# A two-block transformer forward pass: norms' root by Ln, Exp and Newton along the row, two projections around the row sum, and the last GLA head's norm by columns

## The chip, the cores and the metric

One core of one Trainium2 chip runs the kernel in one launch. The metric is device time in microseconds (us); lower is better. The core has TensorE (PE: matmuls, with PEld for loading their stationary operand), VectorE (DVE), ScalarE (ACT: activation functions from tables that are loaded by set), GpSimd (POOL), and DMA queues that SyncE (SP) issues to. TensorE's clock has two levels, 1.2 and 2.4 GHz; the profile's granted clock gives it as a share of the higher.

## The reference

512 tokens of width 1024 pass through two models of two layers each: gated linear attention (GLA) and a convolutional FFN, then native sparse attention (NSA) and a convolutional FFN, a norm, then twice a hybrid of differential and stick-breaking attention and a plain gated FFN, then a last norm. What the change touches is the norm of a vector, with n = 1024 for x, 256 for a head of the GLA, 128 for one of differential attention:

```python
def rmsnorm(x, g):
    x32 = x.astype(jnp.float32)
    y = x32 * lax.rsqrt(jnp.mean(x32 * x32, axis=-1, keepdims=True) + EPS)
    return (y * g).astype(x.dtype)
...
    o = o * lax.rsqrt(jnp.mean(o * o, axis=-1, keepdims=True) + EPS) * g_out      # GLA, per head
    o = o.reshape(Bsz, S, H * DV).astype(h.dtype) * jax.nn.silu(r)
    return o @ w_o
...
    h2 = rms_norm(x, g_ffn)                                                       # plain FFN
    gate, up = jnp.split(h2 @ w_ffn_in, 2, axis=-1)
    return x + (jax.nn.silu(gate) * up) @ w_ffn_out
```

## The kernel before

The residual x lies in SBUF as eight tiles of 128 channels by 512 tokens. Everything is fp32, split into a high and a low part in a reduced format (`hh`/`hl` for x times the norm's gain, `wh`/`wl` for a weight tile `wr`), and a product is three matmuls: high by high (L323), high weight by low data (L324), low weight by high data (L325). A projection to 128 channels is `proj` (L337): 8 blocks of x, 24 matmuls of 128x512 into one PSUM tile `pd`. The weight tiles come by DMA in the order of their use (`wblk`, `wrun`, `_wload`), three raw tiles and three pairs of split ones in flight (PF and WB are 3): ACT casts the high part (L199), DVE subtracts the low one (L200).

A norm's gain goes into `split_norm` ahead of the projection; the root of each token is multiplied in behind it, as `rbc`, a tile whose rows are all the same. So the projections of a norm can run before its root is there, but no output can be evicted without `rbc`. Before the change the root has two forms:

- by columns, for every norm of x: `sqsum` (L409) makes the squares on ACT (L415) and adds them on DVE (L419); `tok_sums` (L422, matmuls L425) sums over the channels, so that a token is a row of a 128x4 tile; `newton` (L396) takes the root in ten operations on DVE (`ms`, `ny`, `nt`: L444, L401 to L406); `bcast` (L427, matmuls L432) turns the columns to `rbc`, which ACT copies out (L435). `rstd` and `rms` put these together.
- by row, for a head of the GLA and of differential attention: `row_rstd` (L447) sums with one matmul (L453, two passes in the profile) so that every row holds the sums, and ACT takes Ln (L455), Exp (L456) and Square (L458), DVE two operations of one Newton step (L459, L460).

`gla` (L605) and `ffn` (L469) start with the norm and one projection ahead (`ahead`), written before the broadcast; `final` (L562) does the last down projection in two halves of 256 tokens, with the last norm by columns for each half (L588, L591, L595, L598), and multiplies the halves (L601). In `gla`, `hnorm` (L702) norms each head's output, then the gate's projections go through Silu (L757, only after the last head's Exp), the product is split (`ohh`, `ohl`), and the output projection follows. The low-rank decay of the GLA passes L629, L630 (`alow`) and the matmul L639.

Instructions are not run in the order in which they are written: a list scheduler with a model of the engines' times fixes each engine's row when the kernel is built, and PSUM banks are given out with it; `after` (L1189) adds an edge that it must keep. At run time each engine takes its row in that order. The rows of engines below are shown as they then stand; a wait in brackets names the engine or DMA queue that a row waits for, and numbers at names only tell tiles apart.

## Time and profile before

| | us |
|---|---|
| median of three runs (lowest, highest) | 2818.37 (2818.32, 2819.44) |
| the profiled execution | 2818.62 |
| its span, first to last instruction | 2816.5 |
| TensorE busy | 2764.6 |
| VectorE busy | 2013.6 |
| ScalarE busy | 1363.8 |
| GpSimd busy | 616.9 |

The profile is of one execution. A timeline row gives the start of an instruction or of a run of like ones, the time from the first's start to the last's end, the engine, the line, the tiles it writes and reads and their shapes; in brackets stands the idle time of the engine before it and what ended that. A matmul's own time overlaps the next one's, so distances between starts count: 0.227 us for 128x512 at 2.4 GHz, 0.43 at 1.2 GHz.

### The profile page before, as it was taken

The numbers are of one execution on the slowest core, as the hardware profiler recorded it, in microseconds if no ns is written. First come the engines' busy times: TensorE is split into PE (matmuls) and PEld (weight loads), VectorE is DVE, ScalarE is ACT, GpSimd is POOL, SyncE is SP. The second block draws the span as 40 slices with busy tenths as digits, with TensorE's granted clock in tenths as the row PEclk, the third lists the DMA queues.
The fourth block names the chain that finished last, engine by engine and source line by source line (L and its number), as shares of the span: only waits on it lengthen the run. The fifth ranks groups of instructions, "written<-read, shape, count | busy, mean of one in ns | idle before, by whom it ended". The sixth has DMA issues, their size and how long they took to land.

```text
span 2816.5 us, 39011 instructions
## 1 busy us (share of the span) xinstructions
PE 2764.6 (98%) x14592; PEld 2339.5 (83%) x14592; DVE 2013.6 (71%) x3105; ACT 1363.8 (48%) x2496; POOL 616.9 (22%) x513
## 2 busy tenths in 40 slices
PE   8999999999999999999999999999999999999998
PEld 6888888888777788888788887899988878889997
DVE  7656755754798875575689768787858896687786
ACT  5444433433486643344477734343436775443333
POOL 4500000001543100000400002466414000056551
PEclk9999999999999999999999999999999999999999
DMA  5222333234621123332422132333323223323331
GB/s 193 68 75 82 98 99 96 98 90 132 155 68 35 61 90 98 97 96 84 117 86 68 60 131 86 98 105 113 113 60 105 76 68 105 120 83 98 105 99 44
DMA packets 102124, 264.55 MB, mean 94 GB/s; under 512 B 13472, under 2 KB 17184, under 8 KB 101936
## 3 DMA queue, kind: packets, MB, share of 16 engines
q1 hardware_dynamic: 101936, 262.07, 29.8%
q8 instruction: 115, 1.88, 0.3%
q14 instruction: 73, 0.60, 0.1%
HBM read 237.93 MB, written 2.10 MB: 85 GB/s over the span
## 4 chain that ended last, share of the span: by engine, by line
PE 89%; DVE 6%; ACT 3%; issue 1%; POOL 1%; DMA 0%; SPq 0%; DVEq 0%; ACTq 0%; POOLq 0%
PE pd L323 20%; PE pd L324 20%; PE pd L325 20%; PE q L323 4%; PE q L325 4%; PE q L324 4%; PE pt L886 2%; PE q L373 1%; PE q L372 1%; PE q L371 1%; PE pa L682 1%; DVE wl L200 1%; DVE ptl L890 1%; PE po L1104 1%; PE pa L871 1%
## 5 line engine op out<-in xcount | busy, mean ns | idle before, releaser
L323 PE MATMUL pd<-hh,wh 128*128 128x512 f32 x1520 | 604.8, 398 | 0.9 <-ACT rbc L435 0.7
L325 PE MATMUL pd<-hh,wl 128*128 128x512 f32 x1520 | 600.7, 395 | 0.0
L324 PE MATMUL pd<-hl,wh 128*128 128x512 f32 x1520 | 600.6, 395 | 0.0
L200 DVE TENSOR_TENSOR wl<-wr,wh 128x1024 fp32r<-128x1024 f32 x309 | 386.3, 1252 | 48.2 <-ACT wh L199 43.3
L199 ACT CAST wh<-wr 128x1024 fp32r<-128x1024 f32 x309 | 320.8, 1045 | 142.2 <-PE pd L324 125.7
L379 DVE TENSOR_TENSOR xl<-yr,xh 128x512 fp32r<-128x512 f32 x322 | 324.4, 1018 | 41.4 <-ACT xh L378 39.8
L323 PEld LDWEIGHTS pd<-hh,wh 128*128 128x128 f32 x1520 | 289.3, 190 | 61.0 <-ACT wh L199 1.5
L325 PEld LDWEIGHTS pd<-hh,wl 128*128 128x128 f32 x1520 | 288.3, 190 | 59.9 <-issue 1.2
L324 PEld LDWEIGHTS pd<-hl,wh 128*128 128x128 f32 x1520 | 289.0, 190 | 58.4 <-issue 0.8
L323 PE MATMUL q<-bbh,xh 128*128 128x256 f32 x952 | 269.4, 283 | 1.5 <-ACT xh L378 1.5
L325 PE MATMUL q<-bbh,xl 128*128 128x256 f32 x952 | 269.4, 283 | 0.0
L324 PE MATMUL q<-bbl,xh 128*128 128x256 f32 x952 | 269.3, 283 | 0.0
L378 ACT CAST xh<-yr 128x512 fp32r<-128x512 f32 x356 | 203.0, 617 | 109.6 <-POOL yr L250 49.2
L773 POOL TENSOR_TENSOR rcos<-al,rbc 128x512 f32<-128x512 f32 x3 | 3.3, 1094 | 931.2 <-ACT rbc L435 931.2
L553 DVE TENSOR_TENSOR x<-pd,x 128x512 f32<-128x512 f32 x84 | 57.6, 689 | 208.3 <-PE pd L325 208.3
L323 PEld LDWEIGHTS q<-bbh,xh 128*128 128x128 f32 x952 | 182.6, 192 | 2.7 <-ACT xh L378 2.0
L324 PEld LDWEIGHTS q<-bbl,xh 128*128 128x128 f32 x952 | 182.6, 192 | 1.0
L325 PEld LDWEIGHTS q<-bbh,xl 128*128 128x128 f32 x952 | 182.6, 192 | 0.8
L275 POOL TENSOR_TENSOR tb<-hn 128x256 f32<-128x256 f32 x8 | 8.1, 1013 | 625.9 <-DVE hn L489 624.5
L324 PE MATMUL pd<-ffl,wh 128*128 128x512 f32 x352 | 136.9, 389 | 0.0
L325 PE MATMUL pd<-ffh,wl 128*128 128x512 f32 x352 | 136.9, 389 | 0.0
L323 PE MATMUL pd<-ffh,wh 128*128 128x512 f32 x352 | 136.3, 389 | 0.0
(402 smaller groups left out, 6138.2 us busy)
## 6 DMA issues: line engine op xcount, KB each, us to landing
wr<-wp SPq DMA_DIRECT2D x309, 512.0 KB, 3.5
yr<-ws SPq DMA_DIRECT2D x136, 256.0 KB, 2.8
yr<-wp SPq DMA_DIRECT2D x118, 256.0 KB, 2.9
sw<-blk SPq DMA_DIRECT2D x80, 64.0 KB, 2.0
x<-xT SPq DMA_DIRECT2D x8, 256.0 KB, 5.2
yr<-cmp_k SPq DMA_DIRECT2D x4, 512.0 KB, 6.4
yr<-cmp_v SPq DMA_DIRECT2D x4, 512.0 KB, 6.9
sw<-qs SPq DMA_DIRECT2D x32, 64.0 KB, 2.0
```

The costliest lines, as they stand in the source:

```text
L199: nc.scalar.copy(hi, raw)
L200: nc.vector.tensor_tensor(lo, raw, hi.bitcast(F), op=OP.subtract)
L323: ins = mm(ps, wh, xh, start=first, stop=False)
L324: mm(ps, wh, xl, start=False, stop=False)
L325: mm(ps, wl, xh, start=False, stop=last)
L371: mm(ps, hh[k][:, tk], wh, start=k == 0, stop=False)
L372: mm(ps, hh[k][:, tk], wl, start=False, stop=False)
L373: mm(ps, hl[k][:, tk], wh, start=False, stop=k == KB - 1)
L378: self.nc.scalar.copy(hi, x)
L379: (eng or self.nc.vector).tensor_tensor(lo, x, hi.bitcast(F), op=OP.subtract)
L553: nc.vector.tensor_tensor(x[n], ps, x[n], op=OP.add)
L886: nc.tensor.transpose(pt[:n, i * P:(i + 1) * P], x, self.ident)
```

## The change

- `row_rstd` takes a finished sum of squares and serves every norm: one matmul with -1, Ln, Exp, Square on ACT, two operations on DVE; no columns, no broadcast. Its matmul is remembered as `last_sum`.
- `columns` makes the token columns (sums and `newton`) beside it only where a token column is needed: `gla` (for v), `rms` in `nsa` and `hyb`. The FFNs need none.
- `headed` starts `gla` and `ffn`: projection 0, the row sum, projection 1, where projection 1's first matmul must come after the sum on TensorE.
- In `hnorm` the heads 0 to 2 keep the row form; the last head goes by columns and broadcast. The gate's Silus now wait for head 2's Exp and the last Exp of the decays (`last_exp`).
- `exp_ln_tables` is called at a head behind a Silu or Sigmoid, in `nsa` and in `final`, and puts the set of Ln and Exp in place. ACT's row has 18 table loads, 11 before.
- `final` takes the row form for each half. Constants move: a tile `minus`, gains without their factor.

```diff
-    def proj(self, name, layer, h, col, tag="pd"):
+    def proj(self, name, layer, h, col, tag="pd", prev=None):
 
         ps = self.psum(tag)
         hh, hl = h
         n = len(hh)
         for k in range(n):
             wh, wl = self.wblk((name, layer, k, col))
-            self.mm3(ps, wh, wl, hh[k], hl[k], k == 0, k == n - 1)
+            ins = self.mm3(ps, wh, wl, hh[k], hl[k], k == 0, k == n - 1)
+            if k == 0 and prev is not None:
+                self.after(ins, prev)
...
+    def row_rstd(self, acc, n, name="rbc", tag="pt"):
+
+
+        nc = self.nc
+        w = acc.shape[1]
+        ps = self.psum(tag)[:, :w]
+        self.last_sum = nc.tensor.matmul(ps, self.minus.to_broadcast([P, P]), acc, start=True, stop=True)
+        y, t = self.g(name)[:, :w], self.g("sq")[:, :w]
+        nc.scalar.activation(y, ps, AF.Ln, scale=-1.0 / n, bias=self.eps)
+        self.root = nc.scalar.activation(y, y, AF.Exp, scale=-0.5)
+        nc.scalar.activation(t, y, AF.Square, scale=(2 * n) ** -0.5)
+        nc.vector.scalar_tensor_tensor(t, ps, -EPS * n, t, op0=OP.add, op1=OP.mult)
+        nc.vector.scalar_tensor_tensor(y, t, 1.5, y, op0=OP.add, op1=OP.mult)
+        return y
...
+    def columns(self, acc, n=D, tag="pt"):
+
+        nc = self.nc
         ps = self.psum(tag)
-        nc.tensor.matmul(ps, self.ones.to_broadcast([P, P]), self.sqsum(xs), start=True, stop=True)
-        y = self.g("ob")
-        nc.scalar.activation(y, ps, AF.Ln, scale=1.0 / n, bias=self.eps)
-        self.root = nc.scalar.activation(y, y, AF.Exp, scale=-0.5)
-        t = self.g("sq")
-        nc.scalar.activation(t, y, AF.Square)
-        nc.vector.scalar_tensor_tensor(t, ps, EPS * n, t, op0=OP.add, op1=OP.mult)
-        nc.vector.scalar_tensor_tensor(y, t, -3.0 * n, y, op0=OP.add, op1=OP.mult)
-        return y
-
-    def rms(self, xs, n=D, name="rbc", tag="pt"):
-
-        y = self.rstd(xs, n, tag)
-        return y, self.bcast([y[:, t:t + 1] for t in range(4)], name, tag)
+        self.tok_sums(acc, ps)
+        a = self.sp.tile([P, 4], F, tag="ms", name="ms", bufs=3)
+        nc.vector.tensor_scalar(a, ps[:, 0:4], 1.0 / n, EPS, op0=OP.mult, op1=OP.add)
+        return self.newton(a, 4)
+
+    def rms(self, xs):
+
+        acc = self.sqsum(xs)
+        r = self.row_rstd(acc, D)
+        return self.columns(acc), r
+
+    def headed(self, x, *ahead):
+
+        if self.last_silu is not None:
+            self.exp_ln_tables()
+        acc = self.sqsum(x)
+        ps = [self.proj(*ahead[0])]
+        r = self.row_rstd(acc, D)
+        ps.append(self.proj(*ahead[1], prev=self.last_sum))
+        return acc, r, ps
...
-        ycol = self.rstd(x)
-        ahead = self.proj(w_up, layer, h, 0)
-        rbc = self.bcast([ycol[:, t:t + 1] for t in range(4)])
+        _, rbc, ahead = self.headed(x, (w_up, layer, h, 0), (w_up, layer, h, FB * P))
...
-                    ps = self.proj(w_up, layer, h, n * P) if n else ahead
+                    ps = ahead.pop(0) if ahead else self.proj(w_up, layer, h, n * P)
...
     def final(self, x, xn, gh, gl, w_down, layer, gname):
 
         nc = self.nc
+        self.exp_ln_tables()
         acc = self.sqsum(xn)
...
-            ps = self.psum("pt")
-            for t in range(2):
-                nc.tensor.matmul(ps[:, t:t + 1], acc[:, a * W + t * P:a * W + (t + 1) * P], self.ones,
-                                 start=True, stop=True)
-            v = self.sp.tile([P, 2], F, tag="fs", name="fs", bufs=2)
-            nc.vector.tensor_scalar(v, ps[:, 0:2], 1.0 / D, EPS, op0=OP.mult, op1=OP.add)
-            y = self.newton(v, 2)
-            ps = self.psum("pt")
-            for t in range(2):
-                nc.tensor.matmul(ps[:, t * P:(t + 1) * P], y[:, t:t + 1].to_broadcast([P, P]), self.ident,
-                                 start=True, stop=True)
-            r = self.g("rbc")[:, :W]
-            nc.scalar.copy(r, ps[:, :W])
+            r = self.row_rstd(acc[:, hs], D)
...
+        acc, rbc, ahead = self.headed(x, ("gla_w_in", 0, h, 0), ("gla_w_in", 0, h, 512))
+        ycol = self.columns(acc)
...
         def hnorm(hd):
-            ob = self.row_rstd(outs[2 * hd:2 * hd + 2], "pa")
+            acc = self.sqsum(outs[2 * hd:2 * hd + 2])
+            if hd < H - 1:
+                ob = self.row_rstd(acc, 256, "ob", "pa")
+            else:
+
+                y = self.columns(acc, 256, "pa")
+                ob = self.bcast([y[:, t:t + 1] for t in range(4)], "ob", "pa")
             for dv in range(2):
                 n = hd * 2 + dv
-                nc.vector.scalar_tensor_tensor(outs[n], outs[n], gain[:, n:n + 1], ob, op0=OP.mult, op1=OP.mult)
+                nc.vector.scalar_tensor_tensor(outs[n], outs[n], self.v("gla_norm", 0, n), ob,
+                                               op0=OP.mult, op1=OP.mult)
...
-            nc.scalar.activation(kd, kd, AF.Exp, scale=-1.0 / 16)
+            last_exp = nc.scalar.activation(kd, kd, AF.Exp, scale=-1.0 / 16)
...
-            self.after(nc.scalar.activation(t, t, AF.Silu), self.root)
+            self.last_silu = nc.scalar.activation(t, t, AF.Silu)
+            self.after(self.last_silu, self.root)
+            self.after(self.last_silu, last_exp)
...
     def nsa(self, x):
         nc = self.nc
         W = 4 * NCMP
+        self.exp_ln_tables()
         ycol, rbc = self.rms(x)
...
-            ob = self.row_rstd([o], "po")
+            ob = self.row_rstd(self.sqsum([o]), P, "ob", "po")
...
             self.after(ins, self.root)
+            self.last_silu = ins
```

In the kernel after, lines have moved: L323 to L325 are L325 to L327, L199/L200 are L201/L202, L425/L432/L435 are L429/L436/L439, L453 to L460 are L457 to L463.

The head of layer 1's conv FFN, TensorE's row. Before, from the last matmuls of projections 0 (`pd_8651`) and 1 (`pd_8695`) to the broadcast:

```order
L324 MATMUL pd_8695<-hl_8602,wh_8504 128x512
L325 MATMUL pd_8695<-hh_8601,wl_8505 128x512
L324 MATMUL pd_8651<-hl_8606,wh_8466 128x512 [waits DVE_49]
L325 MATMUL pd_8651<-hh_8605,wl_8467 128x512
L323 MATMUL pd_8695<-hh_8605,wh_8504 128x512
L425 MATMUL pt_8609<-al_71,sq_8610 128x1 [waits DVE_49]
L425 MATMUL pt_8609<-al_71,sq_8610 128x1 x3
L324 MATMUL pd_8695<-hl_8606,wh_8504 128x512
L325 MATMUL pd_8695<-hh_8605,wl_8505 128x512
L432 MATMUL pt_8682<-al_71,ny_8639 128x128 [waits DVE_49]
L432 MATMUL pt_8682<-al_71,ny_8639 128x128 x3
```

After, from the last matmuls of projection 0 (`pd_8639`) into projection 1 (`pd_8679`):

```order
L326 MATMUL pd_8639<-hl_8608,wh_8472 128x512 [waits DVE_49]
L327 MATMUL pd_8639<-hh_8607,wl_8473 128x512
L325 MATMUL pd_8639<-hh_8611,wh_8472 128x512 [waits Activation_49]
L326 MATMUL pd_8639<-hl_8612,wh_8472 128x512 [waits DVE_49]
L327 MATMUL pd_8639<-hh_8611,wl_8473 128x512
L457 MATMUL pt_8670<-sq_8616,minus_109 128x512 [waits DVE_49]
L325 MATMUL pd_8679<-hh_8583,wh_8510 128x512
L326 MATMUL pd_8679<-hl_8584,wh_8510 128x512
```

Before, the two projections are interleaved, and the last `hl` is used near the end of both; after, projection 0 runs to its end, then comes the sum, then projection 1.

The end of the GLA, ScalarE's row. Before, around the Ln and Exp of the last head (`ob_1409`), the table load and the gate's Silus (`gr`):

```order
L199 CAST wh_1616<-wr_1614 128x1024 [waits DMAHW3_49,PE_49]
L199 CAST wh_1655<-wr_1653 128x1024 [waits DMAHW4_49,PE_49]
L455 ACTIVATE ob_1409<-pa_1402,eps_107 128x512 [waits PE_49]
L456 ACTIVATE ob_1409<-ob_1409 128x512 [waits Activation_49]
L757 ACT_TABLE_LOAD
L757 ACTIVATE gr_1449<-gr_1449 128x512
L757 ACTIVATE gr_1488<-gr_1488 128x512
L757 ACTIVATE gr_1527<-gr_1527 128x512
L757 ACTIVATE gr_1566<-gr_1566 128x512
```

After, around those of head 2 (`ob_1349`); `sq_1404` is a square of the last head:

```order
L459 ACTIVATE ob_1349<-pa_1347,eps_107 128x512 [waits PE_49]
L762 COPY go_1392<-po_1384 128x512 [waits PE_49]
L460 ACTIVATE ob_1349<-ob_1349 128x512 [waits Activation_49]
L771 ACT_TABLE_LOAD
L771 ACTIVATE gr_1468<-gr_1468 128x512
L771 ACTIVATE gr_1507<-gr_1507 128x512
L771 ACTIVATE gr_1546<-gr_1546 128x512 [waits DVE_49]
L771 ACTIVATE gr_1585<-gr_1585 128x512 [waits DVE_49]
L461 ACTIVATE sq_1350<-ob_1349 128x512 [waits Activation_49]
L419 ACTIVATE sq_1404<-go_1392 128x512
L201 CAST wh_1596<-wr_1594 128x1024 [waits DMAHW2_49,PE_49]
```

The table load and the first four Silus have moved in front of the last head's squares.

The head of the first plain FFN, ScalarE's row around the root (`rbc`). Before, with the copy of the broadcast:

```order
L378 CAST xh_15341<-yr_15337 128x512 [waits DMAHW7_49,PE_49]
L378 CAST xh_15345<-yr_15339 128x512 [waits DMAHW0_49,Activation_49]
L199 CAST wh_14947<-wr_14945 128x1024 [waits PE_49]
L435 COPY rbc_14980<-pt_14975 128x512 [waits PE_49]
L533 ACT_TABLE_LOAD
L533 ACTIVATE tp_14982<-tp_14982 128x512 [waits DVE_49]
L265 CAST bbh_15033<-hn_15029 128x256 [waits DVE_49]
```

After, with Ln, Exp and Square (`wh_14961` takes the buffer of `wh_14801`, projection 1's):

```order
L459 ACTIVATE rbc_14951<-pt_14949,eps_107 128x512 [waits PE_49]
L382 CAST xh_15272<-yr_15268 128x512 [waits DMAHW4_49]
L382 CAST xh_15276<-yr_15270 128x512 [waits DMAHW5_49]
L382 CAST xh_15311<-yr_15307 128x512 [waits DMAHW6_49]
L382 CAST xh_15315<-yr_15309 128x512 [waits DMAHW7_49]
L460 ACTIVATE rbc_14951<-rbc_14951 128x512 [waits Activation_49]
L382 CAST xh_15364<-yr_15351 128x512 [waits DMAHW0_49]
L201 CAST wh_14961<-wr_14959 128x1024 [waits PE_49]
L461 ACTIVATE sq_14952<-rbc_14951 128x512 [waits Activation_49]
L554 ACT_TABLE_LOAD
L554 ACTIVATE tp_14989<-tp_14989 128x512 [waits DVE_49]
```

Casts of `xh`, weights of the quads that follow, now stand between the root's steps. On TensorE there, projection 1 (`pd_14958`) is followed by projection 2 (`pd_15049`):

```order
L326 MATMUL pd_14958<-hl_14891,wh_14801 128x512
L327 MATMUL pd_14958<-hh_14890,wl_14802 128x512
L325 MATMUL pd_15049<-hh_14862,wh_14833 128x512
L326 MATMUL pd_15049<-hl_14863,wh_14833 128x512
L327 MATMUL pd_15049<-hh_14862,wl_14834 128x512
```

Projection 2's first matmul stands without a wait of its own, where before its like stood behind the broadcast.

## Rows read from the trace of the kernel before

**Rows 1.** The page, busy us by engine (share of the span), instructions.
```profile
PE 2764.6 (98%) x14592; PEld 2339.5 (83%) x14592; DVE 2013.6 (71%) x3105; ACT 1363.8 (48%) x2496; POOL 616.9 (22%) x513
```

**Rows 2.** Waits of TensorE: line, awaited; us in total, times, longest.
```profile
PE pt L432 <- DVE ny L406: 9.1, 4, 3.1
...
PE pt L595 <- DVE ny L406: 4.7, 1, 4.7
```

**Rows 3.** Windows: us, then busy us (instructions) by engine, granted clock, DMA.
```profile
core 0: us, PE busy (x) PEld busy (x) DVE busy (x) ACT busy (x) POOL busy (x), PEclk, DMA share, GB/s
...
210.00:220.00 10.00, 6.91 (x18) 5.19 (x19) 10.00 (x17) 5.87 (x11) 0.00 (x0) 0.66 0.24 78
...
980.00:990.00 10.00, 8.42 (x29) 7.10 (x30) 5.35 (x14) 4.01 (x5) 0.00 (x0) 0.66 0.18 52
...
1400.00:1410.00 10.00, 7.45 (x29) 5.48 (x28) 8.71 (x14) 5.67 (x13) 8.66 (x7) 0.83 0.69 187
...
1730.00:1740.00 10.00, 8.92 (x30) 7.07 (x31) 7.95 (x12) 5.54 (x9) 4.78 (x5) 0.66 0.00 0
...
2460.00:2470.00 10.00, 9.02 (x37) 7.47 (x38) 7.77 (x14) 4.78 (x8) 4.13 (x4) 0.83 0.01 2
```

**Rows 4.** Groups by line (busy us, mean ns | idle), and one row of the timeline.
```profile
L425 PE MATMUL pt<-al,sq 128*128 128x1 f32 x72 | 8.5, 239 | 0.0
...
L453 PE MATMUL pa<-sq,al 128*128 128x512 f32 x8 | 4.1, 593 | 0.0
...
L456 ACT ACTIVATE ob<-ob 128x512 f32<-128x512 f32 x12 | 7.7, 639 | 0.1
...
1352.74 1.05 PE L432 MATMUL pt<-al,ny 128*128 128x128 f32 x8
```

**Rows 5.** Timeline, GLA's start: start us, us, engine, line, instruction.
```profile
17.15 0.68 DVE L419 TENSOR_TENSOR sq<-sq 128x512 f32<-128x512 f32 x1
...
18.30 0.39 PE L323 MATMUL pd<-hh,wh 128*128 128x512 f32 x1
...
34.58 0.54 PE L323 MATMUL pd<-hh,wh 128*128 128x512 f32 x1
```

**Rows 6.** Timeline, GLA's end: ScalarE, then TensorE, [idle before <-releaser].
```profile
205.71 1.28 ACT L757 ACT_TABLE_LOAD   x1
...
207.01 3.23 ACT L757 ACTIVATE gr<-gr 128x512 f32<-128x512 f32 x6
...
208.95 0.39 PE L325 MATMUL pd<-hh,wl 128*128 128x512 f32 x1
...
211.32 0.73 PE L323 MATMUL pd<-ohh,wh 128*128 128x512 f32 x2 [1.99 <-ACT ohh L378]
...
219.40 0.39 PE L325 MATMUL pd<-ohh,wl 128*128 128x512 f32 x1
```

**Rows 7.** Timeline, head of the conv FFN of layer 1.
```profile
966.97 0.39 PE L323 MATMUL pd<-hh,wh 128*128 128x512 f32 x1
...
973.82 0.74 DVE L385 SCALAR_TENSOR_TENSOR hl<-x,al,hh 128x512 fp32r<-128x512 f32 x1
...
987.26 0.40 PE L323 MATMUL pd<-hh,wh 128*128 128x512 f32 x1
```

**Rows 8.** Timeline, heads of the two plain FFNs.
```profile
1715.51 0.39 PE L323 MATMUL pd<-hh,wh 128*128 128x512 f32 x1
...
1738.31 0.40 PE L325 MATMUL pd<-hh,wl 128*128 128x512 f32 x1
...
2446.93 0.39 PE L323 MATMUL pd<-hh,wh 128*128 128x512 f32 x1
...
2465.41 0.39 PE L325 MATMUL pd<-hh,wl 128*128 128x512 f32 x1
```

**Rows 9.** Timeline, `final`: the products of the two halves on VectorE.
```profile
2803.37 2.96 DVE L601 TENSOR_TENSOR xf<-xf,rbc 128x512 f32<-128x512 f32 x3 [0.23 <-ACT rbc L598]
...
2810.15 2.96 DVE L601 TENSOR_TENSOR xf<-xf,rbc 128x512 f32<-128x512 f32 x3 [1.78 <-ACT rbc L598]
```

**Rows 10.** Windows: NSA's body (columns as in rows 3).
```profile
730.00:960.00 230.00, 225.41 (x1297) 174.97 (x1296) 198.54 (x430) 157.33 (x412) 97.46 (x136) 0.99 0.27 69
```

More of the change, by code (lines that the diff above doesn't have):

```diff
@@ L146, in setup @@
         nc.gpsimd.memset(self.eps, EPS)
+        self.minus = self.small("minus", 1, 1)
+        nc.gpsimd.memset(self.minus, -1.0)
         bf = [al[:, nx + 1 + i * 64:nx + 1 + (i + 1) * 64].bitcast(BF) for i in range(3)]
@@ L445, in rstd @@
         return self.newton(a, 4)
-    def row_rstd(self, xs, tag):
+    def row_rstd(self, acc, n, name="rbc", tag="pt"):
         nc = self.nc
-        n = P * len(xs)
-        ps = self.psum(tag)
-        nc.tensor.matmul(ps, self.ones.to_broadcast([P, P]), self.sqsum(xs), start=True, stop=True)
-        y = self.g("ob")
-        nc.scalar.activation(y, ps, AF.Ln, scale=1.0 / n, bias=self.eps)
-        self.root = nc.scalar.activation(y, y, AF.Exp, scale=-0.5)
-        t = self.g("sq")
-        nc.scalar.activation(t, y, AF.Square)
-        nc.vector.scalar_tensor_tensor(t, ps, EPS * n, t, op0=OP.add, op1=OP.mult)
-        nc.vector.scalar_tensor_tensor(y, t, -3.0 * n, y, op0=OP.add, op1=OP.mult)
-        return y
-    def rms(self, xs, n=D, name="rbc", tag="pt"):
-        y = self.rstd(xs, n, tag)
-        return y, self.bcast([y[:, t:t + 1] for t in range(4)], name, tag)
+        w = acc.shape[1]
[10 more added lines that the diff above has]
+        nc = self.nc
+        ps = self.psum(tag)
+        self.tok_sums(acc, ps)
[14 more added lines that the diff above has]
+        return acc, r, ps
     def ffn(self, x, w_up, w_down, layer, gname, grow, conv, final=None):
@@ L614, in gla @@
         h = self.split_norm(x, "norm_mix", 0)
-        ycol = self.rstd(x)
-        ahead = self.proj("gla_w_in", 0, h, 0)
-        rbc = self.bcast([ycol[:, t:t + 1] for t in range(4)])
+        acc, rbc, ahead = self.headed(x, ("gla_w_in", 0, h, 0), ("gla_w_in", 0, h, 512))
+        ycol = self.columns(acc)
         hh, hl = h
@@ L651, in gla @@
             for which, out in ((0, qs), (1, ks)):
-                ps = self.proj("gla_w_in", 0, h, which * 512 + hd * P) if which or hd else ahead
+                ps = ahead.pop(0) if ahead else self.proj("gla_w_in", 0, h, which * 512 + hd * P)
                 t = self.g("gq")
@@ L698, in gla @@
         outs = []
-        gain = self.small("gain", KB, 1)
-        nc.vector.tensor_scalar(gain, self.v("gla_norm", 0, 0, KB), -1.0 / 512, None, op0=OP.mult)
         def hnorm(hd):
-            ob = self.row_rstd(outs[2 * hd:2 * hd + 2], "pa")
+            acc = self.sqsum(outs[2 * hd:2 * hd + 2])
[4 more added lines that the diff above has]
+                ob = self.bcast([y[:, t:t + 1] for t in range(4)], "ob", "pa")
             for dv in range(2):
                 n = hd * 2 + dv
-                nc.vector.scalar_tensor_tensor(outs[n], outs[n], gain[:, n:n + 1], ob, op0=OP.mult, op1=OP.mult)
+                nc.vector.scalar_tensor_tensor(outs[n], outs[n], self.v("gla_norm", 0, n), ob,
+                                               op0=OP.mult, op1=OP.mult)
         for hd in range(H):
@@ L1232, in hyb @@
         sub = self.small("sub", 1, 2)
-        nc.vector.tensor_scalar(sub, self.v("diff_subln_2", layer, 0), (LAM_INIT[layer] - 1.0) / (2 * P), None, op0=OP.mult)
+        nc.vector.tensor_scalar(sub, self.v("diff_subln_2", layer, 0), 1.0 - LAM_INIT[layer], None, op0=OP.mult)
         def block(col, scale=1.0):
```

## The prediction

> **What bounds the kernel now.** The page's table of engines comes first: TensorE is busy 2764.6 of 2816.5 us [rows 1], so a change can win only what TensorE idles (52 us), what it runs at half clock, and the few matmuls that go. The view of TensorE's waits says where it idles [rows 2]: 9.1 us in four waits of the broadcast L432 for the Newton columns `ny`, 4.7 us once in front of L595 in `final`. The windows say what follows a stall [rows 3]: the granted clock averages 0.66 to 0.83 over 10 us around each, which is 6.8 to 3.4 us at 1.2 GHz in place of 2.4, also at 211, where the waits are of 1.99 us and less [rows 6]. So a stall costs itself and a stretch of matmuls at 0.43 us from start to start in place of 0.227. I measure each place whole: from a matmul that ran at full clock to a later one, less their count times 0.227.
>
> **Prices** [rows 4]. Four token sums: 8.5 us over 9 calls, 0.94 each. Four broadcasts at full clock: 1.05. A row sum L453: 4.1 over 4, 1.03; I take 1.0 for the new one. Ln, Exp and Square about 0.64 each, the two Newton steps about 0.74 each (an operation of that kind and shape, `hl`, is in [rows 7]): about 3.4 us from the sum to the root, less than one projection of 24 matmuls (24 x 0.227 = 5.45).
>
> **Part by part.**
>
> *GLA's start.* Now: projection 1 starts at 18.30 [rows 5], the sums stand inside it, L432 waits for `ny` and L639 for `alow`, projection 3 runs at half clock until its tenth matmul at 34.58. At full clock that equals a start at 34.58 - 9 x 0.227 = 32.54. After: the row sum at 18.30 (the last addition to the squares starts at 17.15 and takes 0.68, so it is there), 1.0; projection 1, 5.45; token sums, 0.94, whose columns only v needs later; L639's successor, as wide as a row sum, some 1.0; projection 3 at 26.7. The root is ready at 18.3 + 1.0 + 3.4 = 22.7, plus DVE's queue. **Gain 5.9** (5.2 to 6.8).
>
> *GLA's end.* From 208.95 to 219.40 lie 16 matmuls, 3.63 us of work: loss 6.8 [rows 6]. The Silus of the gate stand on ACT behind the last head's Ln and Exp, so `ohh` comes 1.99 late, and `ohl` after it. After: the table load and four Silus stand directly behind head 2's Exp, some 60 matmuls before the output projection. The last head's norm goes by columns: its sums 24 matmuls before the end of the gates, its broadcast 15 matmuls into the output projection. Behind the broadcast lie a copy, two products, a cast and a subtraction, some 4.5 us with the queues, against 21 matmuls (4.8 us): it just fits. Extra TensorE work 0.94 + 1.05 - 1.03 = 0.96. **Gain 5.9** (4.9 to 6.1).
>
> *Conv FFN of layer 0.* No wait now; 0.94 + 1.05 becomes 1.0. **Gain 0.9.**
>
> *Conv FFN of layer 1.* From 966.97 to 987.26 lie 57 matmuls, 12.94 us: loss 7.35 [rows 7]. But here the change takes something away. Now projection 1 fills TensorE while DVE still makes the last `hl` (starts 973.82, takes 0.74). After, projection 1 stands behind the sum, and the sum behind all of projection 0. Projection 0's 23rd matmul could start at 966.97 + 22 x 0.227 = 971.96, and its `hl` comes at 974.56: 2.6 us of waiting. DVE's queue in this stretch is the same before and after, so nothing shortens it. Every gap of about 2 us goes with half clock in [rows 3]; 3.4 to 6.8 us of that cost 1.7 to 3.4 at most, since the stall itself lies in part of it, and I take 2.3. Loss after: 1.0 + 2.6 + 2.3 = 5.9. **Gain 1.4** (0.3; 3.7 if the clock stays).
>
> *Plain FFNs.* From 1715.51 to 1738.31 lie 62 matmuls, 14.07: loss 8.73; from 2446.93 to 2465.41 lie 56, 12.71: loss 5.77 [rows 8]. After: 1.0 each. Here every output block of the layer before takes 24 matmuls, so DVE keeps up: last `hl` some 3.3 us, last square some 4.2 us after projection 0 begins, which takes 5.45. The root is late, though: on ACT its Exp stands behind four casts of `xh` and its Square behind a `wh` that needs a buffer projection 1 reads to its end, so the root comes some 4 us after projection 1. Nobody waits for that: projections 2 and 3 (10.9 us) have free banks and stand without a wait on it, and the first consumer, the cast `bbh` of the next products, follows some 1.5 us after the root. **Gains 7.7** (6 to 7.9) **and 4.8** (3.5 to 5).
>
> *Final.* Between the first half's products and the second's lie 6.78 us on DVE [rows 9]: the first half's three (2.96 us), then ten small Newton steps, broadcast and copy. After, the first half's products stand in front of the last eviction (they start near 2801.5), then come a square, two additions, the sum, three half-wide ACT operations and two on DVE, some 4.1 us: the last products start near 2808.7 in place of 2810.15, and TensorE has 0.3 more to do. **Gain 1.2** (0 to 2.5).
>
> *The norms of NSA and the hybrids.* A row sum beside the token sums in place of the broadcast: nothing. But in the first hybrid the second sums and their broadcast go some 22 matmuls (5.0 us) further down the row, and with them the rotated keys and the first scores. There TensorE stands 2.55 of the 10 us from 1400 on, and 3.4 go at half clock [rows 3]: too few projections are left to fill the scores' chain, and later scores leave fewer. Bounds: nothing, and 6 lost (the 5.0 and some clock). I take **2.5 lost**, short of the middle, since some filler follows.
>
> *The attention bodies* come out in another row order. Nothing prices this; in NSA's TensorE idles 4.6 us of 230 [rows 10], so I allow 4 either way.
>
> *Table loads* go from 11 to 18. The load at 205.71 takes 1.28, and the next activation starts at 207.01 [rows 6], nothing behind it. Three new loads stand before the last square of an FFN head, where 1.2 us of slack remain after it. The Trainium skill ("ScalarE: Activation LUTs", section "What ACT_TABLE_LOAD costs") adds a drain of about 1.38 us to the load's 1.28. By that rule the sums of three heads would come about 0.2 us late each, and the time would be 0.6 us above my forecast; the row shows no such gap.
>
> **Sum.** 5.9 + 5.9 + 0.9 + 1.4 + 7.7 + 4.8 + 1.2 - 2.5 = 25.3; 2818.62 - 25.3 = 2793.3 for the profiled run (span and 2.1 around it), 0.25 less by the median of the runs: 2793.1.
>
> **Rivals.**
>
> *The third projection waits for the root after all* at the plain FFNs: then it starts some 4.4 us late and some 2 go at half clock, 6.4 each and 2805.9. For it: projection 0's bank comes free only with the root. Against it: in the new order that projection has no wait of its own. 6%.
>
> *The bodies pay.* The first hybrid loses its 6 and the others 4 to 8 in new waits: 2801 to 2805. For it: late scores, and DVE busy 198.5 of NSA's 230 us [rows 10]. 15%.
>
> *More comes back.* FFN 1 keeps the clock (2.3) and the hybrid loses nothing (2.5), the bodies win a little: 2785 to 2789. 15%.
>
> *Slower.* In NSA's body DVE is the second busiest engine, with 31.5 us free, and TensorE idles 4.6 [rows 10]. If the new row order sets weights' low parts in front of the scores' chain on DVE, TensorE waits there again and again, half clock behind each wait. It decides once the body loses 25.3 us more than now; slower by over 0.2% needs 31, some 35 us of idle time and clock in all, and gives 2824. Against it: the change adds no DVE work to that body. 4%.
>
> *The change doesn't do what it says*: projection 1 does not cover the root because ACT's queue holds Ln back, and half the stalls stay: 2806 to 2815. Against it: at the GLA's and both conv heads Ln, Exp and Square stand in a row. 5%.
>
> **Chances.** Forecast 55%, the others as above. The range holds the forecast, the second and third rivals and the first: 2783 to 2808. 0.2% is 5.6 us, about what a measurement can tell from no change. Faster 0.91, same 0.05, slower 0.04.
>
> **What would show it.** L432's wait for `ny` is gone from TensorE's waits, and 1.2 GHz appears neither at 30, 215, 1735 nor 2465 us; a wait for `hl` of about 2.6 us stands at the head of layer 1's FFN, with 1.2 GHz behind it; in the first hybrid the wait for `pe` has grown past 2.55; the plain FFNs' third projection starts within 0.3 us of the second's end. Wrong if that projection waits for `tp`, if the GLA's output projection still waits for `ohl`, or if the idle time of the bodies moves by more than 6 us.

## Result and profile after

The changed kernel takes 2804.69 us in the median of four runs (2801.44 to 2806.51), the kernel before beside it 2818.35 (2817.47 to 2819.44). The ratio is 0.9945, 95% interval 0.9933 to 0.9957: 0.55% faster. The forecast was 2793.1 in a range of 2783 to 2808. So the sign and the range held, and 11.6 us of the forecast gain of 25.3 did not come, or were given back. The profiled execution took 2801.44, with a span of 2799.4, 17.1 less than before.

This is the page's first part after, as [rows 1]. TensorE is busy 15.6 us less and still fills 98% of the span. Its idle time fell only from 51.9 to 50.4 us: what the GLA and the FFNs gave up in waits, the three attention bodies took (2.9 us more in NSA, 4.3 in the first hybrid, 2.6 in the second). The gain lies in the busy time, that is in fewer matmuls and in matmuls at full clock: the mean granted clock rose from 0.990 to 0.995.

```profile
PE 2749.0 (98%) x14514; PEld 2321.7 (83%) x14514; DVE 2024.9 (72%) x3065; ACT 1397.8 (50%) x2519; POOL 608.6 (22%) x514
```

TensorE's waits after (line, awaited: us in total, times, longest). Neither wait of [rows 2] is left. In their place stand the attention's weights `pe`, `fgl` in the plain FFNs, `hl` in layer 1's FFN, the last sum in `final`, and, in NSA, `ce` (weights of its compressed branch, made on GpSimd). The first row is the start of the program.

```profile
PE po L336 <- DVE wa L623: 7.4, 1, 7.4
PE pa L876 <- ACT pe L1313: 6.3, 7, 2.4
PE pt L902 <- DVE pe L1318: 4.3, 4, 1.5
PE pt L457 <- DVE sq L606: 4.2, 1, 4.2
PE pd L326 <- DVE fgl L383: 3.5, 5, 1.1
...
PE pd L326 <- DVE hl L389: 2.3, 2, 1.4
PE pt L902 <- POOL ce L1070: 1.7, 1, 1.7
```

Windows after (columns as in [rows 3]): at the GLA's end the clock stays whole, at the head of layer 1's FFN and in the first hybrid it does not.

```profile
200.00:210.00 10.00, 10.00 (x49) 8.40 (x48) 5.61 (x15) 2.45 (x4) 0.00 (x0) 1.00 0.33 105
210.00:220.00 10.00, 10.00 (x46) 8.28 (x45) 7.06 (x11) 5.40 (x9) 0.00 (x0) 1.00 0.23 72
...
960.00:970.00 10.00, 9.02 (x31) 6.50 (x32) 5.09 (x8) 4.57 (x7) 0.00 (x0) 0.83 0.33 105
...
1410.00:1420.00 10.00, 7.24 (x44) 5.67 (x42) 9.66 (x18) 8.82 (x22) 0.00 (x0) 0.93 0.40 104
1420.00:1430.00 10.00, 9.66 (x59) 9.11 (x60) 7.06 (x23) 7.41 (x21) 0.00 (x0) 0.73 0.18 54
```

The clearest view is time by stage, from the start of TensorE's first `hh` matmul of a stage to that of the next in the timeline. The GLA runs from the span's start, the tail from the start of the last product of `fg` to the span's end. All later readings use this table (us, one profiled execution each).

| kernel | GLA | FFN 0 | NSA | FFN 1 | hybrid 1 | plain FFN 1 | hybrid 2 | plain FFN 2 | tail |
|---|---|---|---|---|---|---|---|---|---|
| before | 259.54 | 360.92 | 346.51 | 366.46 | 382.08 | 358.43 | 372.99 | 354.56 | 15.01 |
| after | 246.95 | 359.94 | 346.38 | 364.43 | 388.74 | 352.87 | 374.87 | 351.00 | 14.22 |
| e1_after | 247.54 | 359.94 | 351.20 | 364.51 | 388.86 | 352.86 | 376.58 | 352.24 | 14.27 |
| e2_early | 247.44 | 359.94 | 346.25 | 364.40 | 379.49 | 355.37 | 374.58 | 350.71 | 14.22 |
| e3_hyb_old | 246.35 | 359.94 | 352.60 | 364.40 | 381.74 | 353.77 | 372.87 | 350.45 | 14.58 |
| e4_noedge1 | 246.95 | 359.94 | 347.25 | 359.96 | 386.98 | 354.79 | 375.12 | 351.72 | 14.59 |
| e5_head_one | 252.74 | 359.94 | 352.39 | 360.00 | 388.46 | 355.27 | 373.50 | 357.49 | 14.61 |
| e6_head_cols | 257.69 | 362.32 | 357.57 | 367.73 | 388.70 | 359.44 | 374.29 | 356.57 | 14.19 |
| e7_gla_rows | 249.50 | 359.94 | 351.07 | 364.49 | 389.25 | 353.55 | 373.47 | 353.28 | 14.25 |
| e8_early_noedge1 | 247.26 | 359.94 | 346.79 | 359.94 | 377.82 | 353.93 | 373.94 | 351.33 | 14.55 |
| e9_hold | 246.71 | 359.93 | 346.39 | 364.21 | 388.65 | 350.60 | 374.57 | 348.95 | 14.19 |
| e10_three | 245.98 | 359.94 | 349.25 | 360.00 | 377.99 | 350.86 | 372.70 | 350.00 | 13.98 |
| e11_four | 246.59 | 359.93 | 350.60 | 359.94 | 378.34 | 350.59 | 373.47 | 348.27 | 13.67 |

| gain, us | GLA | FFN 0 | NSA | FFN 1 | hybrid 1 | plain FFN 1 | hybrid 2 | plain FFN 2 | tail | sum |
|---|---|---|---|---|---|---|---|---|---|---|
| forecast | 11.8 | 0.9 | 0 | 1.4 | -2.5 | 7.7 | 0 | 4.8 | 1.2 | 25.3 |
| measured | 12.6 | 1.0 | 0.1 | 2.0 | -6.7 | 5.6 | -1.9 | 3.6 | 0.8 | 17.1 |

Of the 8.2 us between these sums, the first hybrid holds 4.2, the plain FFNs 3.4, the second hybrid 1.9, the tail 0.4; the other stages came out 1.6 better. The rest of the 11.6 is that the profiled run of after was its fastest, 2801.44 against a median of 2804.69; where a median run spends these 3.3 us is not shown.

### The profile page after: what moved, and what is told of

Read it like the earlier page. It is cut to its first block, busy times and chain, and to the rows that moved or that the text cites. A ratio compares the mean times of both kernels' runs of the same rounds, so it can differ in the third digit from the quotient of the medians.

```text
span 2799.4 us, 38899 instructions
## 1 busy us (share of the span) xinstructions
PE 2749.0 (98%) x14514; PEld 2321.7 (83%) x14514; DVE 2024.9 (72%) x3065; ACT 1397.8 (50%) x2519; POOL 608.6 (22%) x514
## 5 line engine op out<-in xcount | busy, mean ns | idle before, releaser
L325 PE MATMUL pd<-hh,wh 128*128 128x512 f32 x1536 | 608.1, 396 | 1.4 <-DVE gate L1404 1.3
L327 PE MATMUL pd<-hh,wl 128*128 128x512 f32 x1536 | 603.5, 393 | 0.0
L201 ACT CAST wh<-wr 128x1024 fp32r<-128x1024 f32 x311 | 326.5, 1051 | 408.8 <-PE pd L326 292.0
L202 DVE TENSOR_TENSOR wl<-wr,wh 128x1024 fp32r<-128x1024 f32 x311 | 391.0, 1258 | 134.4 <-ACT wh L201 126.0
L325 PEld LDWEIGHTS pd<-hh,wh 128*128 128x128 f32 x1536 | 289.3, 188 | 62.3 <-issue 3.2
L327 PEld LDWEIGHTS pd<-hh,wl 128*128 128x128 f32 x1536 | 289.1, 188 | 59.4 <-issue 0.9
L327 PE MATMUL q<-bbh,xl 128*128 128x256 f32 x952 | 269.4, 283 | 0.0
L325 PE MATMUL q<-bbh,xh 128*128 128x256 f32 x952 | 269.4, 283 | 0.0
L325 PEld LDWEIGHTS q<-bbh,xh 128*128 128x128 f32 x952 | 182.6, 192 | 0.9
L327 PEld LDWEIGHTS q<-bbh,xl 128*128 128x128 f32 x952 | 182.7, 192 | 0.9
L327 PE MATMUL pd<-ffh,wl 128*128 128x512 f32 x352 | 136.9, 389 | 0.0
L325 PE MATMUL pd<-ffh,wh 128*128 128x512 f32 x352 | 136.3, 389 | 0.0
```

The source lines that it names most:

```text
L201: nc.scalar.copy(hi, raw)
L202: nc.vector.tensor_tensor(lo, raw, hi.bitcast(F), op=OP.subtract)
L325: ins = mm(ps, wh, xh, start=first, stop=False)
L327: mm(ps, wl, xh, start=False, stop=last)
```

## Experiments

All start from the changed kernel and compute all of it; ratios are to the kernel before on the same chip, with 95% intervals.

**e1: the changed kernel again.**

> The changed kernel as it is, once more, as the yardstick for the runs beside it. Both theories: 2801 to 2807 us, 0.994 to 0.996 of the kernel before; the stages from TensorE's first matmul of each: GLA 247, first FFN 360, NSA 346, second FFN 364, first hybrid 389, third FFN 353, second hybrid 375. If its runs lie some 5 us apart, the stage that holds the difference between this profile and the other one of the same kernel tells which part is not steady.

Measured: 2804.60 (2802.59 to 2810.02), ratio 0.9944 (0.9931 to 0.9958). Its profiled run has a span of 2808.0, 8.6 above the other's, of which 4.8 are in NSA, with the same instructions and much the same waits. The last section returns to that. Stage differences of some 5 us in NSA and 1 to 2 us in the second hybrid and second plain FFN are thus no evidence; the other stages repeat within 0.6. Edits elsewhere move a stage too: in e2, e3, e4, e7 and e8, which do not touch them, the first plain FFN takes 353.6 to 355.4 and the second 350.5 to 353.3.

**e2: the first hybrid's second sums early.** Here `y1` and the second `tok_sums` are written ahead of `row_rstd`.

```diff
-            y1, r1 = self.rms(x)
+            acc = self.sqsum(x); y1 = self.columns(acc)
             ps = self.psum("pt")
-            self.tok_sums(self.sqsum(x, gs), ps)
+            self.tok_sums(self.sqsum(x, gs), ps); r1 = self.row_rstd(acc, D)
```

> One edit: in the first hybrid the token sums of the second norm stand in the program ahead of the row sum of the first, so that on TensorE the second sums come 65 matmuls earlier in the row, the broadcast of yc 61 earlier and the first score of the rotated keys 66 earlier. Theory A (the hybrid loses 6.7 us because its second sums, its broadcast and so the rotated keys come late): of the 7 us of waits for pe and ptl between 1390 and 1421 us most vanish, the first hybrid takes 381 to 384 us in place of 388.7, the whole is 5 to 8 us below the changed kernel. Theory B (the scores have too few projections left to stand among, wherever they begin): the same waits move to an earlier or a later place, the first hybrid takes 387 to 391 us, and the whole is within 2 us of the changed kernel.

Measured: 2794.43, ratio 0.9909 (0.9895 to 0.9922). The whole is 10.2 below e1. The first hybrid takes 379.49, 9.4 less than in e1, more than theory A said, and even 2.6 less than before the change. TensorE's waits from 1380 to 1440 us before the change:

```profile
PE pt L886 <- DVE pe L1301: 3.0, 2, 2.5
```

The same place after the change, from 1370 to 1430:

```profile
PE pt L902 <- DVE pe L1318: 3.9, 3, 1.5
PE pa L876 <- ACT pe L1313: 3.0, 3, 2.4
```

And in e2, from 1370 to 1430:

```profile
PE pt L902 <- DVE pe L1318: 1.5, 1, 1.5
PE pa L876 <- ACT pe L1313: 1.3, 3, 0.7
```

The granted clock stays whole through the stage in e2:

```profile
1318.03:1697.52 379.49, 375.21 (x1899) 310.13 (x1898) 289.49 (x482) 236.74 (x462) 40.91 (x26) 1.00 0.31 98
```

Theory A stands: how early the second sums stand in the row sets the stage. The row form itself is not dear there, since e2 keeps it.

**e3: both hybrids' norms in the old form.**

```diff
-            y1, r1 = self.rms(x)
+            y1 = self.columns(self.sqsum(x)); r1 = self.bcast([y1[:, t:t + 1] for t in range(4)])
...
-            ycol, rbc = self.rms(x)
+            ycol = self.columns(self.sqsum(x)); rbc = self.bcast([ycol[:, t:t + 1] for t in range(4)])
```

> The norms of both hybrids in the old form (columns by Newton, then a broadcast of them), all else as changed. Theory A (the row form beside the columns moved the second sums down the row and the weights of the first two heads with them): the first hybrid goes back to 382 us (6.7 less), the second from 374.9 to 373.0, the whole to 8 us below the changed kernel. Theory B (the loss is from the stages around, such as the gates' edge or the load of the tables): the first hybrid stays at 388 us and the whole within 2 us.

Measured: 2794.05, ratio 0.9904 (0.9889 to 0.9918). The whole is 10.5 below e1. The hybrids take 381.74 and 372.87, as before the change (382.08, 372.99). The first hybrid's loss came with its `rms`, not with the stages around. The second's 2.0 us are hardly more than the 1.7 by which e1 differs from after; e11 comes back to it.

**e4: no edge behind the sum in layer 1's FFN.**

```diff
-        ps.append(self.proj(*ahead[1], prev=self.last_sum))
+        ps.append(self.proj(*ahead[1], prev=self.last_sum if edge else None))
...
-        _, rbc, ahead = self.headed(x, (w_up, layer, h, 0), (w_up, layer, h, FB * P))
+        _, rbc, ahead = self.headed(x, (w_up, layer, h, 0), (w_up, layer, h, FB * P), edge=not conv or layer != 1)
```

> Only in the FFN of layer 1 the second projection is no longer held behind the row sum; in the row, 5 of its matmuls then stand among the last 14 of the first projection. Theory A (holding it there costs the two waits for hl, 2.3 us, and the half clock behind them): the waits for hl at 953 to 970 us fall under 0.7 us, the granted clock there stays at 1.0, and the FFN of layer 1 takes 361 to 362.5 us in place of 364.4; the whole is 2 to 3.5 us less than the changed kernel. Theory B (the squares and the additions on VectorE set the row sum's time, so that whatever TensorE does before it, the stage takes the same): within 0.7 us of 364.4.

Measured: 2799.92, ratio 0.9928 (0.9916 to 0.994). The stage takes 359.96, 4.5 less than with the edge, more than either theory said, and the same as layer 0's FFN, which has no wait at all. The window of 10 us from the start of the stage, after the change and then in e4:

```profile
953.27:963.27 10.00, 7.73 (x28) 5.04 (x26) 8.79 (x14) 7.01 (x9) 0.00 (x0) 0.90 0.16 52
```

```profile
953.80:963.80 10.00, 10.00 (x46) 8.27 (x45) 8.61 (x14) 5.97 (x8) 0.00 (x0) 1.00 0.17 52
```

2.27 us of idle time become none. The edge that was to cover the root took away the filler for `hl`.

**e5: the row form, but only one projection written ahead.** The line `ps.append(...)` is left out, for all heads, and the edge goes with it.

> The heads of the GLA and of all four FFNs with the row sum and the root by rows, but only the first projection written ahead of it: the second follows in its turn and may stand before the sum. In the row of the plain FFNs the sum then stands behind 51 matmuls in place of 24, in layer 1's FFN behind 44 in place of 24. Theory A (on TensorE's own row nobody waits for the root, but VectorE's chain behind the root, products of the pairs and low parts of fg, sets when the first products of fg can run): the plain FFNs' root comes some 6 us later, and the first plain FFN takes 356 to 360 us in place of 352.9, with waits for fgl or tp of over 4 us; layer 1's FFN takes 360 as without the edge; the whole is 2802 to 2810. Theory B (only the broadcast's wait counted): the plain FFNs stay at 353 and 351 to 352 us, layer 1's FFN takes 360, the whole is 2799 to 2801.

Measured: 2817.01, ratio 0.9991 (0.9982 to 1.0), above what either theory said: nearly all of the gain is gone. Layer 1's FFN takes 360.00, as in e4. But in the GLA the sum now stands behind 20 more matmuls, and TensorE waits for `alow`; the stage takes 5.8 more. In both plain FFNs the sum stands behind 24 more, and the first matmul of the third projection, right behind it, is released only by the root's Newton step L462. TensorE's waits in e5:

```profile
PE pd L325 <- DVE sq L462: 5.6, 2, 2.8
...
PE pa L648 <- DVE alow L639: 2.5, 1, 2.5
PE q L327 <- DVE xl L383: 2.0, 1, 2.0
```

So in the GLA (5.8) and the plain FFNs (2.4 and 6.5) it pays that projection 1 stands behind the sum and not in front; e5 takes out the edge and the writing ahead together and does not part the two. In layer 1's FFN that order costs. Another 6.0 of e5's loss are in NSA, which the edit does not touch and which differs by 4.8 between two runs of one kernel. Theory A named a consequence of the late root, but the wrong place: the third projection, not the products of `fg`. L462 reads the sum's PSUM bank; that the projection waits for a bank is likely, but the trace names only the releaser.

**e6: two projections, but columns and broadcast.**

```diff
-        r = self.row_rstd(acc, D)
-        ps.append(self.proj(*ahead[1], prev=self.last_sum))
-        return acc, r, ps
+        y = self.columns(acc)
+        ps.append(self.proj(*ahead[1]))
+        return acc, self.bcast([y[:, t:t + 1] for t in range(4)]), ps
```

> The heads with two projections ahead, but with the old norm: sums by token, columns by Newton, a broadcast of them. In the row the broadcast then stands 4 matmuls behind the sums in the GLA, 10 in the first FFN, 2 in layer 1's, 7 in the plain ones. Theory A (the row form pays, since its one matmul waits for no root): the stalls for the columns are back, the GLA takes 5 to 6 us more than changed, layer 1's FFN 364 to 367, the plain ones 357 to 359 and 354 to 356, the whole is 2815 to 2822. Theory B (the second projection pays, whatever the norm's form): every stage stays within 1.5 us of the changed kernel, the whole at 2803 to 2808.

Measured: 2834.15, ratio 1.0055 (1.0039 to 1.0071): slower than before. The wait of [rows 2] now stands in all five heads, in place of four, and is dearer than its 9.1:

```profile
PE pt L436 <- DVE ny L410: 12.9, 5, 3.9
```

Every FFN takes longer than before the change (362.32, 367.73, 359.44, 356.57). The gain of the heads is the row form's, whose one matmul waits for no root; the second projection written ahead gives nothing beside the old norm. But it did not cover the root there: in the row the broadcast stands 2 to 10 matmuls behind the sums. A broadcast held back until the second projection is done was not run. The GLA takes 10.7 more than after, above theory A's 5 to 6, and 11.2 of the loss are in NSA, whose own norm the edit does not touch.

**e7: the last GLA head by rows.**

```diff
-            if hd < H - 1:
+            if hd < H:
```

> The last GLA head's norm by rows like the other three, all else as changed. Theory A (the last head's Ln and Exp hold the Silus of the gates and the casts behind them, so that the output projection waits for ohh and ohl as before): the GLA takes 250 to 253 us in place of 247, with waits for oh of 2 us and more and 1.2 GHz near 210 us; the whole is 3 to 6 us above the changed kernel. Theory B (the Silus stand ready either way, and the columns cost 1 us of matmuls): the GLA takes 246 us, the whole is 0 to 1 us below.

Measured: 2806.78, ratio 0.996 (0.9946 to 0.9974). The GLA takes 249.50, 2.5 more than after, though it has the cheaper sums. TensorE waits for the low part of the last head, with 0.45 for the high part besides; the clock stays whole.

```profile
PE pd L326 <- DVE ohl L383: 1.8, 2, 1.6
```

Theory A by its mechanism, but the stage lies just below its 250 to 253, and the 1.2 GHz that it named did not come: the columns are worth 2.5 us.

**e8: e2 and e4 together.**

> Both edits together: the second token sums of the first hybrid early, and no edge in the FFN of layer 1. If the two gains are independent, the first hybrid takes 379.5 us and layer 1's FFN 360, and the whole is 13.9 us below the changed kernel, about 2791. If they are not (a row order that suits the one and not the other), one of the two stages gives 2 us or more back, and the whole is 2793 to 2798.

Measured: 2789.11, ratio 0.9894 (0.9879 to 0.9908). The two gains add up: 377.82 and 359.94.

**e9: the second quad's low parts later.** From its sixth block on a plain FFN makes gate and up together as a quad: seven products `q` of sums of weight blocks (`yr`, split to `xh` and `xl`) with sums of the normed x. VectorE puts them together in seven steps, L305 to L312, to `qc`, whose split is again `fgh` and `fgl`. In e9 TensorE's row stays the same, matmul by matmul; VectorE's moves, and with it ScalarE's and GpSimd's steps on `qc` come a few casts and sums sooner. `late` is the subtraction that makes the first quad's `fgl`.

```diff
-        (eng or self.nc.vector).tensor_tensor(lo, x, hi.bitcast(F), op=OP.subtract)
+        self.low = (eng or self.nc.vector).tensor_tensor(lo, x, hi.bitcast(F), op=OP.subtract)
+        if late is not None: self.after(self.low, late)
...
-        out = {n: self.split(x, "x") for n, x in ...
+        out = {n: self.split(x, "x", late=self.late) for n, x in ...
```

> The changed kernel with one thing moved on VectorE: in both plain FFNs the low parts of the second quad's six weight sums stand behind the low part of the first quad's fg, not among the seven steps that make it. TensorE's row is the same, matmul by matmul. Theory A (what is missing of the plain FFNs' gain is VectorE's queue, which now stands in front of the first products of fg, since TensorE comes 6.7 us closer to it): the two waits for fgl in the first plain FFN, 1.6 us, and those of the second, 1.9 us, fall under 0.5 each, these FFNs take 351.3 and 349.5 us, the whole is 2 to 3.5 us below the changed kernel. Theory B (the low part waits for the q products or for the cast on ScalarE, not for VectorE's queue): the waits for fgl stay, and the stages within 0.4 us of 352.9 and 351.0. If the six low parts are then late themselves, waits for xl appear at the second quad's products in place of those for fgl.

Measured: 2797.41, ratio 0.9922 (0.9907 to 0.9937). The plain FFNs take 350.60 and 348.95, 2.3 and 2.05 less than after; the first has no wait left, the second 0.6. In e10 and e11, with the same edit, they take 350.9 and 350.0, 350.6 and 348.3, all below every run without it. The median is 7.3 below the changed kernel's, the profiled span 5.2, so the whole fell by more than these stages show. VectorE's timeline after: between the first step on the `q` products (L305) and `fgl` stand `xl` after `xl`.

```profile
1772.94 0.42 DVE L305 TENSOR_TENSOR qu<-q,qu 128x256 f32<-128x256 f32 x1
1773.27 1.67 DVE L383 TENSOR_TENSOR xl<-yr,xh 128x512 fp32r<-128x512 f32 x1
1774.87 0.68 DVE L383 TENSOR_TENSOR fgl<-tp,fgh 128x512 fp32r<-128x512 f32 x1
...
1775.80 1.44 DVE L383 TENSOR_TENSOR xl<-yr,xh 128x512 fp32r<-128x512 f32 x1
...
1781.31 1.38 DVE L383 TENSOR_TENSOR xl<-yr,xh 128x512 fp32r<-128x512 f32 x1 [0.61 <-ACT xh L382]
1782.83 1.55 DVE L383 TENSOR_TENSOR fgl<-qc,fgh 128x512 fp32r<-128x512 f32 x1
```

In e9 they come behind it, and 9.9 us from L305 to the last `fgl` become 6.4, and all of the difference is in the seven steps (7.16 us, then 3.65):

```profile
1771.30 0.42 DVE L305 TENSOR_TENSOR qu<-q,qu 128x256 f32<-128x256 f32 x1
1772.07 0.69 DVE L382 TENSOR_TENSOR fgl<-tp,fgh 128x512 fp32r<-128x512 f32 x1 [0.35 <-ACT fgh L382]
...
1777.67 0.69 DVE L382 TENSOR_TENSOR fgl<-qc,fgh 128x512 fp32r<-128x512 f32 x1 [2.72 <-ACT fgh L382]
1778.28 11.60 DVE L382 TENSOR_TENSOR xl<-yr,xh 128x512 fp32r<-128x512 f32 x10
```

Theory A: the missing gain of the plain FFNs stood in VectorE's queue.

**e10: e2, e4 and e9 together.**

> Three edits on the changed kernel: the second token sums of the first hybrid early, no edge in layer 1's FFN, the second quad's low parts held back. TensorE's row is that of the first two edits together. If the gains add up: what these two gave (2789.1 median) less the 2 to 3.5 us of the third, 2785.5 to 2787. If the third moves its wait elsewhere: 2788 to 2791.

Measured: 2782.03 (2779.98 to 2787.26), ratio 0.9867 (0.9850 to 0.9884): 1.3% faster than before, and clear of the change's own interval, 0.9933 to 0.9957. That is more than the sum expected.

**e11: e10 with the second hybrid's norm in the old form.**

> The same three edits, and the norm of the second hybrid in its old form (columns and their broadcast). Theory A (the row form costs the second hybrid 1.9 us, since the scores then come 25 matmuls sooner in the row, before the keys are ready): the second hybrid takes 372.9 us, 1 to 2 us less than with the three edits. Theory B (that difference was chance): within 0.7 us of them.

Measured: 2783.17, ratio 0.9865 (0.9851 to 0.988). The second hybrid takes 373.47, with the row form in e10 372.70. Theory A's size falls: the old form is 0.8 slower here, not 1 to 2 faster. The stage's time also moves by distant edits (372.7 to 376.6 in the table). But TensorE's idle time in it does go with the form: 2.9 to 3.3 us in the three profiles with the old one (before, e3, e11), 3.9 to 5.7 in the ten with the row form. So the form has a part in the loss, and what else in the row decides it stays open.

## Why the prediction was right and wrong

**GLA.** This part was right. The sum starts at 18.90, the third projection at 27.14 (forecast 18.3 and 26.7), 5.4 us before the equal of its start before [rows 5]; 5.9 was forecast. TensorE's timeline after:

```profile
18.90 1.02 PE L457 MATMUL pt<-sq,minus 128*128 128x512 f32 x2
...
27.14 0.50 PE L325 MATMUL pd<-hh,wh 128*128 128x512 f32 x1
```

The other 7.2 of the stage's 12.6 hold the end's 5.9 and a wait of 1.03 for `gd`, a tile of the decays, at 83 us that went too. "It just fits" was right: no wait for `oh`, and e7 prices the columns at 2.5.

**FFN 0, FFN 1.** In FFN 0 the prices give 0.94 + 1.05 - 1.0 = 0.99, where the prediction wrote 0.9; 0.98 was measured. FFN 1 was right in mechanism: waits for `hl` of 0.84 and 1.42, 2.3 in all, where 2.6 was forecast, and half clock behind them. Their cost was forecast as 2.6 + 2.3 and is 4.5 by e4. What the prediction did not draw is that the wait came from the edge alone.

**Plain FFNs.** The stalls were sized right: 7.7 and 4.8 were forecast, and with VectorE's queue cleared they give 7.8 and 5.6 (e9 against before). Of the 5.6, a wait of 1.5 is not the broadcast's: it stood 40 us into the stage before, outside what was priced, and went too. Without it 4.1 came, with 0.6 of other waits left in e9.

```profile
2487.09 0.38 PE L323 MATMUL q<-bbh,xh 128*128 128x256 f32 x1 [1.53 <-ACT xh L378]
```

The step that failed is the sentence that nobody waits for the late root. It was checked for TensorE's next projections and for the first consumer, not for the chain behind it. In the first plain FFN TensorE reached its first product of `fg` 65.4 us into the stage in place of 73.3, 7.8 sooner; VectorE's first product with `rbc` came at 15.6 in place of 16.8, only 1.2 sooner, with the same 51.6 us from there to L305 (51.5 before), of which VectorE works 46.6. That a sooner root would have cured it too is argued and was not run; e9 shows the cure in the queue. TensorE had run 6.6 us closer to VectorE, and 1.6 (1.8 in the second) came back as waits for `fgl`. The root was late for the reason given, ScalarE's casts between Ln and Exp, and the table load in the head has nothing behind it. ScalarE's timeline:

```profile
1708.12 1.28 ACT L1185 ACT_TABLE_LOAD   x1
1709.41 0.63 ACT L419 ACTIVATE sq<-x 128x512 f32<-128x512 f32 x1
...
1717.31 0.63 ACT L460 ACTIVATE rbc<-rbc 128x512 f32<-128x512 f32 x1
...
1719.31 0.62 ACT L461 ACTIVATE sq<-rbc 128x512 f32<-128x512 f32 x1
```

The Trainium skill ("ScalarE: Activation LUTs", section "What ACT_TABLE_LOAD costs") has a drain of about 1.38 us beside the load; here the load starts 0.02 us behind the instruction before it and the square 0.01 us after the load's end, so the measurement decides, and the forecast without a drain was right.

**The rival on the third projection** did not come true, but it is real: with the sum 24 matmuls further down the row, e5 shows 2.8 us of it in each plain FFN.

**First hybrid.** The prediction was right in cause and place, wrong in size, and outside its bounds of 0 to 6: 6.7 were lost. The failed step is "short of the middle, since some filler follows". The scores are a chain of short products, and the delay of its start came back nearly whole: 4.3 us more idle time, and half clock behind it (0.93 and 0.73 above). e2 shows the other direction, which the prediction did not see: those sums could stand earlier than before.

**NSA.** Forecast 0, measured 0.1, but by luck. TensorE idles 9.4 us there in place of 6.5, and 9.0 to 11.9 in every profile after the change; most of it is, in the profiled run, one new wait of 1.7 for `ce`, new waits of 1.3 for a weight pair, and 0.9 more for `pe`, less 1.3 that went at `qs`. In the profiled run the clock made up for it (0.985 before, 0.995 after); in e1 it did not (0.981), and NSA lost 4.7. No run puts NSA's old norm back, so whether its row form, its table load or the row order brings the wait stays open.

**Second hybrid.** Forecast 0, measured 1.9 lost, inside the 4 either way. Its idle time grew by 2.6; the form has a part in it, the rest is not settled (e11).

**Tail.** 0.8 in place of 1.2, inside its bounds. The last sum waits 4.2 us for the squares of the last block, whose eviction stands on VectorE behind the first half's three products (2.96 us), as forecast; from the one half's products to the other's lie 7.8 us, where 7.2 were forecast.

**Among the rivals**, the measured median lies in "the bodies pay" (2801 to 2805). Its first part came true. Its second part, losses of 4 to 8 in the other bodies, did not in the profiled run (1.9, and the plain FFNs gave the rest), but did in e1's (4.7 and 3.6). One of the three signs of being wrong came, too: the idle time of the bodies moved by more than 6 us, by 2.9, 4.3 and 2.6. So the time fell inside the range, at its slow side, with the heads and the GLA's end as forecast and 8.5 lost in the three attention stages, where the sum had 2.5. "L432's wait is gone" and no half clock at 30, 215, 1735 and 2465 us were right. "The wait for `pe` has grown past 2.55" was right only for the sum: 6.9 us in six waits in place of 3.0, the longest 2.4.

## What to carry over

In the plain FFNs a stall that went was paid in full only once the engine that comes next was earlier too: compare how much sooner each engine reaches the meeting point, and put work that is not yet due behind the meeting, not in front. A sum whose matmul needs no root takes the wait off TensorE's row, a second projection written around a broadcast did not, as the rows came out. An order that holds filler back must be weighed at each place of use, since the second projection behind the sum was worth 5.8 us in the GLA's head and cost 4.5 in an FFN's. And a stage that comes out as forecast can hide a new wait: look at its idle time and its clock, not only at its sum.

## What the hardware showed

In NSA the granted clock fell at different places in two executions of the same program, with nearly the same idle time in front. Three windows of NSA after, 110, 120 and 180 us into the stage:

```profile
716.89:726.89 10.00, 8.12 (x51) 6.93 (x50) 4.40 (x11) 3.23 (x9) 8.35 (x8) 1.00 0.53 131
726.89:736.89 10.00, 10.00 (x48) 7.31 (x46) 7.89 (x12) 4.18 (x8) 6.63 (x8) 1.00 0.92 222
786.89:796.89 10.00, 10.00 (x76) 8.74 (x75) 9.92 (x29) 8.90 (x31) 8.62 (x16) 1.00 0.09 22
```

The same three in e1:

```profile
717.42:727.42 10.00, 8.10 (x44) 7.09 (x42) 3.63 (x7) 3.29 (x10) 8.41 (x8) 0.86 0.52 129
727.42:737.42 10.00, 10.00 (x36) 7.28 (x36) 5.17 (x13) 2.93 (x5) 5.58 (x6) 0.80 0.82 202
787.42:797.42 10.00, 9.32 (x44) 7.72 (x44) 7.95 (x23) 6.93 (x24) 8.21 (x14) 0.66 0.35 81
```

TensorE is busy 8.1 us in the first window of both, at 1.00 in the one and 0.86 in the other; over the stage that is 346.4 against 351.2 us. In both the longest gap in front is the wait for `ce`, 1.74 us, 116 us into the stage. Eight more of the kernels above have that wait, at 1.74 to 1.76 us; over the 20 us from 110 us into the stage the granted clock is 1.00 in three of the ten and 0.83 to 0.92 in seven. Why it fell in some and not in others was not found. A stage with idle time of this kind has no single time, and two profiles of one kernel are needed before a few us there are read as an effect.
